# Key tiles of the last token group and the gates beside them, moved from one PSUM tag to another

## The chip, the cores and the metric

The kernel runs on one core of a Trainium2 chip. The metric is the device time of one execution in microseconds (us), given as the median of several executions. A profile of one execution records what each engine did: TensorE (PE in the profile, its weight loads PEld), VectorE (DVE), ScalarE (ACT), GpSimd (POOL) and SyncE (SP), which here issues the DMAs.

## What is computed

The program is a trunk of two layers over 1024 latent tokens and 256 context tokens of width 1024. Cut to what matters here, a layer is:

```python
h = _rms(x) * (1 + scale) + shift            # hc likewise for the context tokens
fa, za, u, vs, zb, q, k, va, zc, g = _split_proj(h @ w_in[l])
q = _axial_rope(_qk(q, N_HEADS, q_norm_g[l]), row, col)
k = _axial_rope(_qk(k, N_KV_HEADS, k_norm_g[l]), row, col)
attn = _latent_attn(q, k, va, kc, vc, attn_sink[l])       # window of 3 blocks, the context, a sink
ga, gb, gc = jnp.split(jax.nn.sigmoid(g), 3, axis=-1)
merged = ga * (ya @ w_pa) + gb * (yb @ w_pb) + gc * (yc @ w_pc)
x = x + gate * (merged @ w_out)
```

ya and yb come from a Fourier mixer and a gated mixer that the change doesn't touch. The context tokens go through the first layer in full, and in the second give keys and values alone.

## The kernel before, in words

**Products.** Every product of a layer's input with a weight is made of three matmuls per block of 128 input channels (L237 to L239, `mm3`), since both operands are split into a high and a low part. A product over 1024 channels is therefore 24 matmuls. `proj_tm` (L246) makes a tile of 128 tokens by 256 columns, `proj_cm` (L241) one of 128 columns by up to 512 tokens. A weight is loaded as a granule (L207): a DMA into a buffer `raw` (two of them), a cast on ACT into `whi` (L212) and a subtraction on DVE into `wlo` (L213); there are five buffers each of `whi` and `wlo`, and a new granule waits until the last matmul on the granule whose buffer it takes.

**PSUM.** A product needs one of eight banks. The pool of line 98 gives them out by tag: two for `mm` (products), three for `s` (scores), two for `pt` (transposes) and one for `o`. `bank(tag)` takes a tile of a tag. A tile whose tag has no free bank waits until all that read and write the tile before it in that bank are done; this holds up the first matmul into it, and PE issues in order, so all that stands behind it waits too.

**The stage in question** is the first part of `attention` (L462 to L496), once in each layer. It goes over three token groups: the context ("C", 256 tokens), then "0" and "1" (512 tokens each). Each block of 128 tokens gets a *key tile*: `proj_tm`, then `qk_norm_rope` (L306) on the key half and two reads of the value half (L484 on ACT, L485 on DVE). `qk_norm_rope` is a long chain through four engines: squares on ACT with the result back in the same bank (L311), scale and power on POOL (L312, L313), a multiplication on DVE that reads the bank (L316), the rotation on POOL and DVE (L325 to L336), and a transpose on PE (L486). The bank comes free with L316, L484 and L485. The input `H[g]` of a group is made just before (`modulate`, L272), in the first layer and, for the last group, in the second.

Beside the key tiles stand two other things. Before the last group ("1"), two *query tiles* are made (`prepare`, L455, `queries`, L435): they take `mm` banks and hold them much longer, since the transposed queries come back into the same bank (L441) and are read from there by ACT and DVE (L446, L447). And `early` (L465) gives *gates made ahead* (`ahead`, L634): `proj_cm`, a tanh on ACT that reads the bank (L644), a DMA of the result to DRAM (L645). In the first layer one follows each key tile, nine in all, of 256 context tokens; in the second there are four of 256 tokens, beside the last group alone.

After the stage come the units of attention: scores into `s` banks (L362 to L371), maxima on DVE, exponentials on ACT (L378, L379), the division on POOL (L387), transposes into `pt` (L399), values into `o` (L406, L407), with more products on `mm` as fill, three more gates among them (`lead`, L617).

**Who sets the order.** The program is written in this order, but each engine's queue is filled by a scheduler when the program is built. It keeps an estimate of its own of when each bank comes free, so a change of tags moves instructions on all engines.

**Which bank a tile takes.** The tiles of the stage that matter: key tiles alternate between the two tags (L479: `bank("mm" if ib % 2 else "s")`), and `ahead` always takes `mm` (L641). So the two `mm` banks serve the two query tiles, half of the key tiles and all gates made ahead.

Of the kernel before, what the change touches and what calls it, by code (L numbers as in the profile page):

```python
# [20 lines left out]
CTX = 256  # L21
# [45 lines left out]
def trunk_kernel(ctx: ExitStack, tc: tile.TileContext, a: dict, out: bass.AP):  # L67
# [17 lines left out]
    def bank(tag):  # L85
        tags = banks["tags"]
        tag = tag if tag in tags else "g"
        return banks["pool"].tile([128, 512], F32, tag, bufs=tags[tag])
# [127 lines left out]
    def w_cm(l, c0):  # L216

        return granule(a["w_in"][l, :, c0:c0 + 128].rearrange("(k p) c -> p k c", p=128), [128, KC, 128])
# [22 lines left out]
    def proj_cm(o, wg, h, n):  # L241

        for k in range(KC):
            mm3(o[:, :n], wg[0][:, k, :], wg[1][:, k, :], h[0][k], h[1][k], k == 0, k == KC - 1)

    def proj_tm(o, wt, h, t0):  # L246

        for k in range(KC):
            wh, wl = wt[k // 4]
            mm3(o[:, 0:256], h[0][k][:, t0:t0 + 128], h[1][k][:, t0:t0 + 128],  # L250
                wh[:, k % 4, :], wl[:, k % 4, :], k == 0, k == KC - 1)
# [167 lines left out]
    def attention(l, groups, sideA, sideB, xp, wkv, X, S):  # L419
# [13 lines left out]
        blocks = [(g, GROUPS[g][0] // 128 + i) for g in groups for i in range(GROUPS[g][1] // 128)]  # L433
# [21 lines left out]
        def prepare(u):  # L455
            kv, g, t, pr = units[u]
            if (kv, t) not in Q:
                if kv not in W:
                    W[kv] = w_tm(a["w_in"][l], C_Q + kv * 256)
                Q[kv, t] = queries(W[kv], g, t)  # L460

        wt = wkv or w_tm(a["w_in"][l], C_KV)  # L462
        ib = 0
        names = ("C", "0", "1")
        early = Fill(before_work(l, groups, S, se["pool"]))  # L465
        if X:
            modulate(l, "C", X["C"], xp)
        for ig, g in enumerate(names):
            if ig == 2:
                prepare(0)  # L470
                prepare(2)
            if X and ig < 2:
                modulate(l, names[ig + 1], X[names[ig + 1]], xp)
            g0, n = GROUPS[g]
            pk = bank("pt")
            for i in range(n // 128):
                t = g0 // 128 + i
                ib += 1
                p = bank("mm" if ib % 2 else "s")  # L479
                proj_tm(p, wt, H[g], i * 128)  # L480
                kf = qk_norm_rope(p, 2, 2, rope, None if g == "C" else t, np_)
                pv = p[:, 128:256].rearrange("p (g d) -> p g d", g=2)

                ACT.mul(vt[:, t, :, 0:64], pv, 0.5)  # L484
                DVE.scalar_tensor_tensor(vt[:, t, :, 64:128], pv, 0.5, vt[:, t, :, 0:64].bitcast(F32), ALU.mult, ALU.subtract)  # L485
                PE.transpose(pk[:, i * 128:(i + 1) * 128], kf[:, 0:128], ident)  # L486
                if "C" in groups:
                    early.upto(early.done + 1)
                elif ig == 2:
                    early.upto(early.done + 1)  # L490
            for kv in range(2):
                src = pk[kv * 64:(kv + 1) * 64, :n]
                hi = kk[0:64, kv, g0:g0 + n]
                ACT.copy(hi, src)
                DVE.tensor_tensor(kk[64:128, kv, g0:g0 + n], src, hi.bitcast(F32), ALU.subtract)
# [6 lines left out]
        st = Pool(tc, name="sd", bufs=1, side=sideB)  # L502
# [41 lines left out]
    def stored(S, key, n):  # L544
        S[key] = dp.tile([128, n], F32, "d" + "_".join(map(str, key)))
        return S[key]

    def staged(st, n=512):
        if st is not se["pool"]:
            return st.tile([128, 512], F32, "st", bufs=stores["n"])[:, :n]  # L550
        return st.tile([128, CTX], F32, "se", bufs=2)[:, :n]
# [69 lines left out]
    def before_work(l, groups, S, st):  # L621

        if "C" in groups:
            return ahead(l, context_blocks(range(9)), S, st)
        return ahead(l, [(b, 1, "0") for b in (0, 2)], S, st, CTX)

    def few(gen, n):
        for _ in range(n):
# [2 lines left out]
    def context_blocks(r):  # L631
        return [(i % 3, i // 3, "C") for i in r]

    def ahead(l, blocks, S, st, part=None):  # L634

        for b, j, g in blocks:
            w = w_cm(l, C_G + b * D + j * 128)
            o = stored(S, ("T", b, j, g), GROUPS[g][1])
            n = part or GROUPS[g][1]
            for c in range(0, GROUPS[g][1], n):  # L640
                p = bank("mm")  # L641
                proj_cm(p, w, [[y[:, c:c + n] for y in x] for x in H[g]], n)
                s = staged(st, n)
                ACT.activation(s, p[:, :n], AF.Tanh, scale=0.5)  # L644
                nc.sync.dma_start(o[:, c:c + n], s)  # L645
                yield n
# [333 lines left out]
    for l in range(DEPTH):  # L980
# [6 lines left out]
        S = {}  # L987

        wkv = None if l else wkv
        attention(l, groups, A, B, xp, wkv, None if l else X, S)  # L990
        stores["n"] = 5
        if not last:
            bigs["C"].close()
        st = Pool(tc, name="st", bufs=1, side=A)
# [5 lines left out]
        blocks = [(b, 0, g) for b in (0, 2) for g in lat]  # L1000
# [130 lines left out]
```

## Time and profile before

| | |
|---|---|
| time, median of 3 executions (lowest, highest) | 1948.63 us (1947.56, 1950.77) |
| the profiled execution's own time | 1947.46 us |
| its span in the profile | 1945.7 us |
| busy: PE, PEld, DVE, ACT, POOL | 1888.2, 1639.1, 1083.1, 798.4, 610.6 us |
| mean granted TensorE clock | 0.992 |
| idle time of PE in the whole span | 1945.7 - 1888.2 = 57.5 us |

A row of the waits view reads "who waited <- for whom: us in total, times, longest". A timeline row reads "start, duration, engine, line, operation, out<-in, how often [idle before <- what ended it]". In a row of the windows view the engines' busy times stand in the order of its heading, each with its number of instructions, and after them the granted clock. Names of tiles are the program's, without their numbers. The stage lies at about 43 to 145 us in the first layer and at about 1097 to 1160 us in the second.

### The profile page before, as it was taken

Reading aid. Unit: us, or ns where it says so; the run is one execution under the profiler, and the core shown is the slowest. Engines: PE = TensorE matmul, PEld = TensorE weight load, DVE = VectorE, ACT = ScalarE, POOL = GpSimd, SP = SyncE. Lnnn points to the kernel's source line nnn. Section 1 sums busy time; section 2 is a strip of 40 time slices with the busy share of each in tenths; the row PEclk is TensorE's granted clock in tenths of the full one; section 3 lists DMA queues with packets and bytes.
Section 4 is the critical chain, followed back from the end, with each engine's and each line's share of the span. In section 5 each row is a group of like instructions: output and inputs, shape, how many; then the busy total and the mean of one; then the engine's idle time right before and its main releaser. Section 6 shows DMA issues by size and latency. Waiting matters only on the chain.

```text
span 1945.7 us, 31000 instructions
## 1 busy us (share of the span) xinstructions
PE 1888.2 (97%) x10975; PEld 1639.1 (84%) x10975; DVE 1083.1 (56%) x2175; ACT 798.4 (41%) x2088; POOL 610.6 (31%) x975
## 2 busy tenths in 40 slices
PE   7889999999999999999999989999999999999998
PEld 2888999999988887888878978899888888888887
DVE  4565665556655548766355556666665655622242
ACT  2654555445644422111243445555554443111221
POOL 1564344443231112121124454334432021211122
PEclk9999999999999999999999999999999999999999
DMA  9332122213554667554374412112124568633362
GB/s 331 105 101 64 50 68 61 72 47 95 162 185 152 191 214 244 164 171 148 120 259 152 136 55 66 57 59 84 34 87 152 155 194 264 201 93 98 127 220 103
DMA packets 270610, 259.77 MB, mean 134 GB/s; under 512 B 20792, under 2 KB 213496, under 8 KB 270456
## 3 DMA queue, kind: packets, MB, share of 16 engines
q1 hardware_dynamic: 270456, 257.80, 41.9%
q8 instruction: 86, 1.41, 0.3%
q14 instruction: 68, 0.56, 0.1%
HBM read 196.91 MB, written 60.83 MB: 132 GB/s over the span
## 4 chain that ended last, share of the span: by engine, by line
PE 82%; DMA 6%; DVE 5%; ACT 3%; issue 2%; POOL 2%; SPq 1%; POOLq 0%; ACTq 0%; DVEq 0%
PE mm L237 16%; PE mm L238 16%; PE mm L239 16%; PE s L238 6%; PE s L237 6%; PE s L239 6%; PE pt L399 3%; DMA raw<-in_w_in_dram 2%; PE o L407 2%; PE o L406 2%; PE s L371 2%; PE s L364 1%; PE s L365 1%; DVE wlo L213 1%; DMA lt<-dT 1%
## 5 line engine op out<-in xcount | busy, mean ns | idle before, releaser
L213 DVE TENSOR_TENSOR wlo<-raw,whi 128x1024 fp32r<-128x1024 f32 (+2 forms) x210 | 243.3, 1161 | 216.3 <-ACT whi L212 207.5
L212 ACT CAST whi<-raw 128x1024 fp32r<-128x1024 f32 (+2 forms) x210 | 202.7, 967 | 363.7 <-PE s L238 139.2
L237 PE MATMUL mm<-hh,whi 128*128 128x512 f32 (+1 forms) x752 | 292.4, 389 | 5.6 <-DVE st L562 3.8
L238 PE MATMUL mm<-hl,whi 128*128 128x512 f32 (+1 forms) x752 | 291.1, 387 | 0.0
L239 PE MATMUL mm<-hh,wlo 128*128 128x512 f32 (+1 forms) x752 | 290.7, 387 | 0.0
L237 PE MATMUL mm<-whi,hh 128*128 128x256 f32 (+1 forms) x704 | 217.6, 309 | 8.1 <-DVE qt L447 5.2
L685 POOL TENSOR_TENSOR m<-m,tb 128x512 f32<-128x512 f32 x64 | 87.1, 1363 | 412.0 <-DVE tb L684 367.6
L239 PE MATMUL mm<-whi,hl 128*128 128x256 f32 (+1 forms) x704 | 214.7, 305 | 0.0
L238 PE MATMUL mm<-wlo,hh 128*128 128x256 f32 (+1 forms) x704 | 214.7, 305 | 0.0
L237 PEld LDWEIGHTS mm<-hh,whi 128*128 128x128 f32 x752 | 141.3, 188 | 33.3 <-DVE st L562 4.7
L239 PEld LDWEIGHTS mm<-hh,wlo 128*128 128x128 f32 x752 | 141.3, 188 | 27.3
L238 PEld LDWEIGHTS mm<-hl,whi 128*128 128x128 f32 x752 | 141.4, 188 | 25.6
L237 PEld LDWEIGHTS mm<-whi,hh 128*128 128x128 f32 x704 | 135.5, 192 | 14.7 <-issue 5.6
L387 POOL TENSOR_SCALAR P<-P,rd 128x640 f32<-128x640 f32 (+2 forms) x144 | 115.0, 809 | 102.1 <-DVE rd L385 63.9
L238 PEld LDWEIGHTS mm<-wlo,hh 128*128 128x128 f32 x704 | 135.7, 193 | 5.0
L239 PEld LDWEIGHTS mm<-whi,hl 128*128 128x128 f32 x704 | 135.4, 192 | 4.8
L238 PE MATMUL s<-hl,whi 128*128 128x512 f32 x352 | 137.5, 391 | 0.0
L237 PE MATMUL s<-hh,whi 128*128 128x512 f32 x352 | 137.4, 390 | 0.0
L239 PE MATMUL s<-hh,wlo 128*128 128x512 f32 x352 | 137.2, 390 | 0.0
L269 DVE TENSOR_TENSOR pl<-pt,ph 128x512 fp32r<-128x512 f32 (+1 forms) x184 | 112.0, 615 | 27.4 <-ACT ph L268 25.0
L268 ACT CAST ph<-pt 128x512 fp32r<-128x512 f32 (+1 forms) x184 | 95.8, 535 | 28.0 <-PE o L406 15.8
L196 DVE SCALAR_TENSOR_TENSOR aacc<-araw,scol,aacc 128x256 f32<-128x256 f32 x196 | 102.2, 554 | 5.1 <-DMA araw<-in_w_ada_dram 2.7
(303 smaller groups left out, 4435.0 us busy)
## 6 DMA issues: line engine op xcount, KB each, us to landing
raw<-in_w_in_dram SPq DMA_DIRECT2D x122, 512.0 KB, 4.1
araw<-in_w_ada_dram SPq DMA_DIRECT2D x48, 512.0 KB, 6.0
raw<-in_w_out_dram SPq DMA_DIRECT2D x40, 512.0 KB, 3.8
dP<-st SPq DMA_DIRECT2D x64, 256.0 KB, 2.3
lp<-dP SPq DMA_DIRECT2D x64, 256.0 KB, 4.2
x<-in_x_dram SPq DMA_DIRECT2D x16, 512.0 KB, 8.6
raw<-in_w_pc_dram SPq DMA_DIRECT2D x32, 256.0 KB, 2.9
dM<-m SPq DMA_DIRECT2D x32, 256.0 KB, 3.4
```

The costliest lines, as they stand in the source:

```text
L196: DVE.scalar_tensor_tensor(acc[:, v, :], raws[k // 4][:, k % 4, :], sc, acc[:, v, :], ALU.mult, ALU.add)
L212: ACT.copy(hi, raw)
L213: DVE.tensor_tensor(lo, raw, hi.bitcast(F32), ALU.subtract)
L237: PE.matmul(o, lh, rh, start=start, stop=False)
L238: PE.matmul(o, lh, rl, start=False, stop=False)
L239: PE.matmul(o, ll, rh, start=False, stop=stop)
L268: ACT.copy(hi, src)
L269: DVE.tensor_tensor(lo, src, hi.bitcast(F32), ALU.subtract)
L371: PE.matmul(bc[:, h * 256:h * 256 + 256], qt[:, s, 2 * pr + h, :], kk[:, g, SEQ:NTOK], start=(h + s == 0), stop=(s == 1), skip_group_check ...
L387: POOL.tensor_scalar(P[hh][:, :nl + 256], P[hh][:, :nl + 256], rd[:, hh:hh + 1], 1.0, ALU.mult, ALU.mult)
L399: PE.transpose(b[:, (2 * i + hh) * 128:(2 * i + hh + 1) * 128], P[hh][:, (i0 + i) * 128:(i0 + i + 1) * 128], ident)
L685: POOL.tensor_tensor(m, m, s, ALU.add)
```

## The change

The key tiles of the last group all take the tag `s`, and so do the gates that `before_work` hands out (nine in the first layer, four in the second). The gates made ahead elsewhere (`lead`, and those after attention) keep `mm`. No product, weight, DMA or reader is added or taken away.

```diff
-                p = bank("mm" if ib % 2 else "s")
+                p = bank("mm" if ib % 2 and ig < 2 else "s")
...
         if "C" in groups:
-            return ahead(l, context_blocks(range(9)), S, st)
-        return ahead(l, [(b, 1, "0") for b in (0, 2)], S, st, CTX)
+            return ahead(l, context_blocks(range(9)), S, st, tag="s")
+        return ahead(l, [(b, 1, "0") for b in (0, 2)], S, st, CTX, "s")
...
-    def ahead(l, blocks, S, st, part=None):
+    def ahead(l, blocks, S, st, part=None, tag="mm"):
...
-                p = bank("mm")
+                p = bank(tag)
```

What this does to the queues, at three places. A tile keeps its number when it changes its tag: 1027 and 1072 are the first layer's query tiles; 1118, 1197, 1276 and 1355 its key tiles of the last group; 1169, 1248 and 1327 the last three of its nine gates. In the second layer 12720 and 12772 are the query tiles, 12825, 12904, 12976 and 13055 the key tiles, 12876, 12948, 13027 and 13099 the gates.

First, PE in the first layer, around the transposes of the first query tile (L441), before:

```order
L239 MATMUL mm_1072<-whi_1023,hl1C_294 128x256
L486 MATMUL pt_694<-ident_69,qf_964 128x128
L441 MATMUL mm_1027<-ident_69,qf_1061 128x128 x2
L237 MATMUL mm_1118<-whi_243,hh01_602 128x256
L238 MATMUL mm_1118<-wlo_244,hh01_602 128x256
L239 MATMUL mm_1118<-whi_243,hl01_604 128x256
```

and now:

```order
L238 MATMUL s_1248<-hl0C_293,whi_1243 128x256
L239 MATMUL s_1248<-hh0C_291,wlo_1244 128x256
L441 MATMUL mm_1027<-ident_69,qf_1061 128x128 x2
L237 MATMUL s_1248<-hh1C_292,whi_1243 128x256
L238 MATMUL s_1248<-hl1C_294,whi_1243 128x256
L239 MATMUL s_1248<-hh1C_292,wlo_1244 128x256
```

Before, the key tile 1118 stands right behind L441 and takes the bank that the query tile leaves; now 1118 stands 120 matmuls earlier, and L441 lies inside a gate.

Second, PE in the second layer, at the same transposes, before:

```order
L239 MATMUL mm_12772<-whi_12716,hl10_11963 128x256
L362 LDWEIGHTS identb_74
L362 MATMUL s_13196<-maskb_87,identb_74 128x128
L486 MATMUL pt_12527<-ident_69,qf_12648 128x128
L486 MATMUL pt_12527<-ident_69,qf_12692 128x128
L441 MATMUL mm_12720<-ident_69,qf_12754 128x128 x2
L237 MATMUL mm_12825<-whi_12438,hh01_12328 128x256
L238 MATMUL mm_12825<-wlo_12439,hh01_12328 128x256
```

and now:

```order
L238 MATMUL s_12948<-hl00_11962,whi_12871 128x256
L239 MATMUL s_12948<-hh00_11960,wlo_12872 128x256
L441 MATMUL mm_12720<-ident_69,qf_12754 128x128 x2
L237 MATMUL s_12948<-hh00_11960,whi_12871 128x256
L238 MATMUL s_12948<-hl00_11962,whi_12871 128x256
```

The first scores (L362) and the key tile 12825 are no longer next to L441; a key tile and most of a gate now stand between the end of the second query tile and L441.

Third, ACT in the first layer, where a gate hands its bank to a key tile (the gate 1248, then the key tile 1276), before:

```order
L212 CAST whi_1437<-raw_1435 128x1024
L311 ACTIVATE mm_1276,s2_1301<-mm_1276 128x64
L311 ACTIVATE s_1355,s2_1380<-s_1355 128x64
L644 ACTIVATE se_1273<-mm_1248 128x256
L409 COPY ot_1623<-o_1609 64x256
```

and now:

```order
L446 CAST qt_1065<-mm_1027 64x2x128 x2
L212 CAST whi_1322<-raw_1320 128x1024
L644 ACTIVATE se_1273<-s_1248 128x256
L311 ACTIVATE s_1197,s2_1222<-s_1197 128x64
L484 ACTIVATE vt_283<-s_1118 128x2x64
```

Before, the gate and the key tile lay in different banks, and the reading of the gate's tile (L644) stood behind the key tile's own squares; now the cast of the next gate's weights (L212) stands just ahead of it, and the next key tile's first matmul stands right behind the gate's last on PE.

## The prediction

> **What bounds the kernel now.** The page comes first.
>
> ```profile
> span 1945.7 us, 31000 instructions
> PE 1888.2 (97%) x10975; PEld 1639.1 (84%) x10975; DVE 1083.1 (56%) x2175; ACT 798.4 (41%) x2088; POOL 610.6 (31%) x975
> PE 82%; DMA 6%; DVE 5%; ACT 3%; issue 2%; POOL 2%; SPq 1%; POOLq 0%; ACTq 0%; DVEq 0%
> ```
>
> PE works for 97% of the span and is 82% of the chain that ended last. The change alters no product, so the time can move in two ways alone: by PE's idle time, and by the clock at which its matmuls run. The windows view shows both. Its first two rows hold the stage in each layer; the other three are single products.
>
> ```profile
> core 0: us, PE busy (x) PEld busy (x) DVE busy (x) ACT busy (x) POOL busy (x), PEclk, DMA share, GB/s
> 75.00:165.00 90.00, 79.41 (x611) 76.11 (x611) 53.73 (x126) 48.51 (x157) 52.70 (x101) 0.98 0.30 89
> 1125.00:1160.00 35.00, 27.47 (x204) 26.01 (x203) 19.90 (x58) 14.59 (x60) 20.20 (x47) 0.90 0.14 43
> 109.80:114.50 4.70, 4.70 (x27) 4.70 (x28) 0.31 (x1) 0.00 (x1) 1.46 (x3) 0.64 0.00 0
> 1136.00:1141.60 5.60, 5.42 (x28) 5.38 (x28) 0.57 (x3) 0.38 (x2) 1.36 (x4) 0.58 0.00 0
> 1127.50:1130.60 3.10, 3.09 (x26) 3.04 (x27) 1.50 (x7) 0.16 (x2) 2.78 (x7) 1.00 0.00 0
> ```
>
> PE is idle for 90.00 - 79.41 = 10.6 us in the first layer's stage and for 35.00 - 27.47 = 7.5 us in the second's, 18.1 us together. No other engine is busy for more than 60% there, and the DMA share is 0.30 and 0.14. So this is waiting, and PE's waits in these two stretches say for whom:
>
> ```profile
> PE mm L237 <- DVE qt L447: 2.6, 1, 2.6
> PE s L371 <- ACT P L379: 2.3, 1, 2.3
> PE mm L441 <- DVE qf L336: 2.2, 1, 2.2
> PE mm L237 <- DVE st L562: 1.1, 1, 1.1
> PE mm L237 <- DVE vt L485: 1.0, 1, 1.0
> PE mm L441 <- POOL qf L321: 0.8, 1, 0.8
> PE mm L237 <- ACT se L644: 0.6, 1, 0.6
> ...
> PE mm L237 <- DVE qt L447: 3.8, 2, 2.6
> PE mm L441 <- ACT kk L494: 2.2, 1, 2.2
> PE mm L237 <- DVE vt L485: 0.9, 2, 0.7
> PE mm L237 <- DVE ta L334: 0.3, 1, 0.3
> PE pt L486 <- DVE qf L336: 0.3, 1, 0.3
> ```
>
> Seven rows are the first layer's, five the second's. The form "PE mm L237" is the first matmul of a product on an `mm` bank. It waits for the last reader of the tile before it there: L447 is a query tile's, L485 a key tile's, L644 a gate's. Two timelines of PE show the largest:
>
> ```profile
> 106.98 0.27 PE L441 MATMUL mm<-ident,qf 128*128 128x128 f32 x1
> 109.81 0.50 PE L237 MATMUL mm<-whi,hh 128*128 128x256 f32 x1 [2.55 <-DVE qt L447]
> 110.11 0.41 PE L238 MATMUL mm<-wlo,hh 128*128 128x256 f32 x1
> ...
> 1133.13 0.41 PE L441 MATMUL mm<-ident,qf 128*128 128x128 f32 x2 [2.18 <-ACT kk L494]
> 1136.18 0.56 PE L237 MATMUL mm<-whi,hh 128*128 128x256 f32 x1 [2.65 <-DVE qt L447]
> ```
>
> In both layers a key tile takes the bank that a query tile has just left. PE transposes the queries (L441), ACT and DVE read them, and PE has nothing it may do until then.
>
> **What the change takes away.** The order answers for each wait.
>
> - *Query tile to key or gate* (2.6 and 3.8 us): key tiles of the last group and gates no longer use `mm`. In the new order the transposes L441 lie inside a gate, and no product within 80 instructions behind them needs the banks of the two early query tiles. Gone: 6.4 us.
> - *Waits for the query chain before L441* (0.8, 2.2 and, in the second layer, 2.2): the first layer's early query tile now has 120 instructions of PE between its last product and its L441 where it had 36, the later one 68 where it had 36. The second layer's has 119 where it had 87: the two that come in between are a key tile and most of a gate, and in the trace the rotated queries were ready at 1133.13, when PE now still works on these. At 3.10 / 26 = 0.119 us each, from the last row of the windows, 68 are 8.1 us. Gone: 5.2 us.
> - *The score behind L379* (2.3): the second context score took the bank of the first; now it takes a gate's, whose last matmul lies 32 instructions back. Gone: 2.3 us.
> - *Gates and key tiles behind a gate or a key tile on `mm`* (0.6 and 1.0 in the first layer; 0.9 - 0.7 = 0.2, 0.3 and 0.3 in the second): these are on three banks now with more distance. Gone: 2.4 us.
> - *Kept*: L562, a fill product that the change doesn't touch (1.1 us), and the 0.7 us wait of the second query tile for L485 in the second layer, up to which both orders agree.
>
> That is 6.4 + 5.2 + 2.3 + 2.4 = 16.3 us of idle time. The clock adds to it. After the two longest stops a product ran at a granted clock of 0.64 and 0.58. At 0.119 us each the 27 and 28 matmuls would have taken 3.2 and 3.3 us instead of 4.70 and 5.42: 1.5 + 2.1 = 3.6 us lost. I count this as gone with the stops: together 19.9 us.
>
> The Trainium skill, "TensorE: Matmul & The Clock Gate", section "What's actually happening", lets the clock drop only after an idle window of about 3.4 us. By that rule the stops of 2.55 and 2.65 us are too short to be the cause and the 3.6 us would stay. The rows speak against it, since both low stretches begin with the product right behind the stop; but 2.3 and 2.2 us stops had none.
>
> **What it adds.** The work of 13 gates and four of the eight key tiles moves to three `s` banks. New waits arise where the new order puts a tile closely behind the last matmul of the tile whose bank it takes. What it would wait for:
>
> ```profile
> 121.53 1.04 ACT L212 CAST whi<-raw 128x1024 fp32r<-128x1024 f32 x1
> 122.47 0.39 ACT L644 ACTIVATE se<-mm 128x256 f32<-128x256 f32 x1
> ...
> 114.13 0.28 PE L239 MATMUL mm<-whi,hl 128*128 128x256 f32 x1
> ...
> 117.96 0.28 DVE L485 SCALAR_TENSOR_TENSOR vt<-mm,vt 128x128 fp32r<-128x128 f32 x1
> ```
>
> A gate's bank comes free after 0.39 us of L644. But two gates have the next gate's cast (L212, 1.04 us) ahead of L644 on ACT, and that cast itself waits for the gate's last matmul: two granules of key weights and two of query weights hold four of the five buffers. The 0.6 us row above was waited for one L644, so a hand-over takes about 0.2 us beside it. Such a bank therefore comes free 1.04 + 0.39 + 0.2 = 1.6 us after the last matmul. A key tile's bank comes free about 118.24 - 114.41 = 3.8 us after its last matmul when nothing stands before it, 32 matmuls. The order has these close ones:
>
> - gate 1248 to key tile 1276, no distance: 1.6 us.
> - gate 1169 to key tile 1197, 8 instructions (1.0 us) between: 0.6 us.
> - a lead gate to a fill product on the same `mm` bank, 9 between, cast ahead: 0.5 us; that fill product to a query tile, 10 between: 1.1 us, the price of the L562 row.
> - later in the first layer, one fill product to the next, 6 between: 0.9 us by the same row.
> - second layer: one lead gate to a query tile, 8 between, with a cast ahead: 0.9 us. Key tile 12825 to 12976 has 80 matmuls (9.5 us) between, but its L485 now stands behind the queries' L447 on DVE: 0.3 us.
>
> Sum 5.9 us. From below each may be nothing, for the tiles' readers may run ahead of my reckoning; from above each may cost what the worst hand-over of the trace costs, 2.65 us, 18.6 us for seven. I take the sum, as the causes are those of its rows. ACT's squares of key tiles (L311) queue behind the casts, but the banks they hold are wanted 52 instructions later or more, 6.2 us against 3.8.
>
> **The queues.** The gates' DMAs move with them. SP meets one obstacle:
>
> ```profile
> 99.02 0.37 SPq L209 DMA_DIRECT2D raw<-in_w_in_dram  x1
> 121.45 0.34 SPq L427 DMA_DIRECT2D gain<-in_k_norm_g_dram  x1
> 122.88 0.36 SPq L645 DMA_DIRECT2D dT_C<-se  x1
> 123.85 0.38 SPq L209 DMA_DIRECT2D raw<-in_w_in_dram  x1
> ```
>
> The second layer's key gain waits 22 us for the last rotation table on POOL, with weight loads behind it. In the new order four issues that stood behind it stand ahead of it, two weight loads among them. The next load is wanted by ACT's cast before the first exponentials.
>
> ```profile
> raw<-in_w_in_dram SPq DMA_DIRECT2D x122, 512.0 KB, 4.1
> ```
>
> A load lands 4.1 us after its issue, and the DMA share in the stage is 0.30: I cost the queue at nothing. What covers it is 87 instructions, 10.4 us, that PE has in the new order between the first context score and the first L399. If a load came late by more than that, the exponentials behind the cast, and PE, would wait for the rest of it.
>
> **The sum.** 19.9 - 5.9 = 14.0 us. The profiled execution took 1947.46 us (span 1945.7 and 1.8 around it), so it would take 1933.5. The median of the runs is 1.2 us higher, 1948.63, so I predict 1934.6 us.
>
> **Rivals.**
>
> *The clock is not bound to these stops* (chance 0.13). For it: the stops of 2.3 and 2.2 us had no low clock, and the low stretches may fall elsewhere. Then 3.6 us less are gained: 10.4 us, 1938.2 us. The Trainium skill's rule on the clock gate, quoted above, would come out here.
>
> *What was waited for at the bank comes back at the softmax* (0.18). The first scores of each layer now stand behind all key tiles; the stage's fill is used up before them, and the chain from scores to L399 lies bare. For it: the new order does put the first layer's first context score 100 PE instructions later. Against: 10.4 us of matmuls still stand between it and L399. Should the chain take 5 us longer than that in each layer, 10 of the 14.0 us go back: 1944.6 us. Two thirds of this chance lie within 0.2% of no change.
>
> *The three `s` banks become the bound* (0.08, slower). Some 21 tiles of the two stages (thirteen gates, eight key tiles) now hand over `s` banks, while `mm` stands idle behind two query tiles. If each hand-over cost the 1.6 us reckoned for an adjacent gate, that is 33.6 us against 19.9 gained: 13.7 us slower, 1962.3 us. It turns at 19.9 / 21 = 0.95 us each. Against: most have 24 or more matmuls between. The Trainium skill, "Perfetto Trace Analysis", section "Matmuls", would have independent products rotate through different banks so that the reading of one overlaps the next; fewer banks for more products goes against it.
>
> That the change does nothing is excluded by the order.
>
> **How the numbers follow.** The forecast itself, a gain of about 8 to 20 us, has 0.61. A measurement of this kernel can tell about 0.2%, 3.9 us, from no change. Faster: 0.61 + 0.13 + 0.06 = 0.80; same: 0.12; slower: 0.08. The low end, 1927, is all of 19.9 us with the kept 1.8 gone too and no new wait; the high end, 1944, takes in new waits of about 15 us, near the bound, and leaves out most of the softmax rival and the slower one.
>
> **What would show it right or wrong.** Right: PE's idle time in the two stages falls from 18.1 to about 8 us; no wait "PE mm L237 <- DVE qt L447" is left there; new rows "PE s L237 <- ACT se L644" of 1 to 2 us appear; no granted clock under 1 in the stage. Wrong: waits of PE for P (L399) or for scores' banks (L362, L371) of several us at the end of the stage; rows "PE s L237 <- DVE vt L485" repeated; or the low clock at other places with the stops gone.

## The result, and the profile after

| | before | after |
|---|---|---|
| time, median of 4 executions each (lowest, highest) | 1948.62 us (1947.56, 1950.77) | 1930.79 us (1928.94, 1933.80) |
| ratio to before, 95% interval | | 0.9909 (0.9892 to 0.9925) |
| the profiled execution, its span | 1947.46, 1945.7 us | 1932.49, 1930.7 us |
| idle time of PE in the span | 57.5 us | 1930.7 - 1884.7 = 46.0 us |
| mean granted TensorE clock | 0.992 | 0.995 |

The kernel is 17.8 us faster; 14.0 were forecast. Two unaltered copies, run later with the experiments, gave 0.9919 and 0.9915. Two single executions of kernels further down took far longer than all others (6601.22 us with the queries moved, 2045.28 us with all key tiles on `mm`); the medians given there contain them, the ratios leave them out.

The page of the kernel after: span, engines, and the shares of the chain that ended last.

```profile
span 1930.7 us, 31006 instructions
PE 1884.7 (98%) x10975; PEld 1636.6 (85%) x10975; DVE 1083.1 (56%) x2175; ACT 796.3 (41%) x2088; POOL 608.5 (32%) x975
PE 81%; DMA 8%; DVE 4%; POOL 2%; ACT 2%; issue 2%; SPq 1%; POOLq 0%; DVEq 0%; ACTq 0%
```

The number of instructions of PE is the same. Its busy time fell by 1888.2 - 1884.7 = 3.5 us (the clock), its idle time by 11.5 us. The windows view of the kernel after, for the stage in the first layer and in the second; the columns are those of the heading in the prediction:

```profile
75.00:160.00 85.00, 81.07 (x612) 77.18 (x611) 53.80 (x126) 44.94 (x151) 53.16 (x102) 0.98 0.31 94
1116.00:1151.00 35.00, 33.31 (x255) 31.64 (x255) 23.81 (x62) 16.45 (x59) 22.06 (x47) 1.00 0.29 85
```

The first row holds as many PE instructions as the 90 us of before (612 against 611), the second 255 where 35 us of before held 204. PE is idle for 85.00 - 81.07 = 3.9 and 35.00 - 33.31 = 1.7 us: 5.6 us where there were 18.1, in the second layer over more work than before. The waits view of the kernel after says for what, the first five rows in the first layer (75 to 165 us), the other three in the second (1107 to 1160 us):

```profile
PE s L237 <- ACT se L644: 1.7, 1, 1.7
PE pt L399 <- POOL P L387: 1.3, 1, 1.3
PE o L406 <- ACT ph L268: 0.3, 1, 0.3
PE s L371 <- ACT P L379: 0.2, 1, 0.2
PE o L407 <- DVE pl L269: 0.2, 1, 0.2
...
PE mm L237 <- DVE vt L485: 0.9, 1, 0.9
PE s L237 <- DVE vt L485: 0.8, 1, 0.8
PE mm L441 <- DVE nm L375: 0.6, 1, 0.6
```

"PE mm L237 <- DVE qt L447", 6.4 us in three stops before, is in neither stretch. The score behind L379 went from 2.3 to 0.2 us, and of the waits before L441 one of 0.6 us is left, of a query tile that is not one of the early ones. Two new stops are over 1 us, and the timeline of the kernel after shows both:

```profile
109.31 1.04 ACT L212 CAST whi<-raw 128x1024 fp32r<-128x1024 f32 x1
110.38 0.38 ACT L644 ACTIVATE se<-s 128x256 f32<-128x256 f32 x1
110.82 0.39 PE L237 MATMUL s<-whi,hh 128*128 128x256 f32 x1 [1.68 <-ACT se L644]
...
138.43 2.06 POOL L387 TENSOR_SCALAR P<-P,rd 128x256 f32<-128x256 f32 x2
138.96 0.34 PE L399 MATMUL pt<-ident,P 128*128 128x128 f32 x1 [1.26 <-POOL P L387]
```

The first is the forecast's largest new wait, gate 1248 to key tile 1276: the cast of the next gate's weights stands ahead of the tanh on ACT, and 1.68 us pass where 1.6 were reckoned. The second was not in the sum: PE is through with its fill and waits for the division of the softmax.

**Where the 17.8 us lie.** To compare the two kernels over the same work I take two stretches between places that both orders share: from PE's 65th matmul to its 1727th (the first layer's stage and what surrounds it), and from the 6465th to the 7575th (the second's), counted in the order of time. Before:

```profile
37.05:280.67 243.62, 227.82 (x1663) 213.12 (x1663) 150.54 (x348) 138.46 (x422) 120.59 (x221) 0.98 0.31 92
1115.72:1287.90 172.18, 163.05 (x1113) 148.82 (x1112) 107.49 (x264) 92.95 (x312) 78.29 (x153) 0.98 0.21 63
```

and after:

```profile
36.07:272.94 236.87, 228.25 (x1663) 212.74 (x1663) 150.97 (x347) 137.49 (x424) 118.12 (x221) 0.98 0.32 96
1107.05:1270.95 163.90, 160.21 (x1112) 146.65 (x1111) 107.50 (x264) 92.66 (x313) 79.16 (x153) 1.00 0.22 66
```

In the second layer 172.18 - 163.90 = 8.3 us went: idle time from 9.13 to 3.69 (5.4 us), and busy time from 163.05 to 160.21 (2.8 us), with the granted clock up from 0.98 to 1.00. In the first layer 6.8 us went: idle time fell by 7.2 us (15.80 to 8.62), and busy time rose by 0.4. Together these are 15.0 us. The first stretch also begins 1.0 us sooner (36.07 for 37.05), the work between the two stretches took 0.9 us less, and what follows the second took 2.0 us more, so the two profiled executions differ by 15.0 us in all. The remaining 2.8 us of the 17.8 lie in which executions were profiled: that of before was 1.2 us under its median and that of after 1.7 us above. The experiments show that the first was lucky in its first layer.

### The profile page after: what moved, and what is told of

It reads as the page before. It is cut to its first block, busy times and chain, and to the rows that moved or that the text cites. A ratio compares the mean times of both kernels' runs of the same rounds, so it can differ in the third digit from the quotient of the medians.

```text
span 1930.7 us, 31006 instructions
## 1 busy us (share of the span) xinstructions
PE 1884.7 (98%) x10975; PEld 1636.6 (85%) x10975; DVE 1083.1 (56%) x2175; ACT 796.3 (41%) x2088; POOL 608.5 (32%) x975
## 4 chain that ended last, share of the span: by engine, by line
PE 81%; DMA 8%; DVE 4%; POOL 2%; ACT 2%; issue 2%; SPq 1%; POOLq 0%; DVEq 0%; ACTq 0%
PE mm L237 15%; PE mm L238 15%; PE mm L239 15%; PE s L238 6%; PE s L237 6%; PE s L239 6%; PE pt L399 3%; DMA raw<-in_w_in_dram 2%; PE o L406 2%; PE o L407 2%; PE s L371 2%; PE s L364 1%; PE s L365 1%; DVE wlo L213 1%; DMA lt<-dT_C 1%
## 5 line engine op out<-in xcount | busy, mean ns | idle before, releaser
L213 DVE TENSOR_TENSOR wlo<-raw,whi 128x1024 fp32r<-128x1024 f32 (+2 forms) x210 | 243.1, 1160 | 218.4 <-ACT whi L212 213.4
L212 ACT CAST whi<-raw 128x1024 fp32r<-128x1024 f32 (+2 forms) x210 | 202.7, 967 | 374.1 <-PE s L238 146.2
L237 PE MATMUL mm<-hh,whi 128*128 128x512 f32 x720 | 284.2, 395 | 2.9 <-DVE st L562 2.7
L238 PE MATMUL mm<-hl,whi 128*128 128x512 f32 x720 | 282.8, 393 | 0.0
L239 PE MATMUL mm<-hh,wlo 128*128 128x512 f32 x720 | 282.6, 392 | 0.0
L237 PE MATMUL mm<-whi,hh 128*128 128x256 f32 (+1 forms) x672 | 206.6, 307 | 2.2 <-ACT st L644 1.1
L239 PE MATMUL mm<-whi,hl 128*128 128x256 f32 (+1 forms) x672 | 204.4, 304 | 0.0
L238 PE MATMUL mm<-wlo,hh 128*128 128x256 f32 (+1 forms) x672 | 204.1, 304 | 0.0
L237 PEld LDWEIGHTS mm<-hh,whi 128*128 128x128 f32 x720 | 135.8, 189 | 30.4 <-DVE st L562 3.9
L238 PE MATMUL s<-hl,whi 128*128 128x512 f32 (+1 forms) x384 | 146.8, 382 | 0.0
L237 PE MATMUL s<-hh,whi 128*128 128x512 f32 (+1 forms) x384 | 146.7, 382 | 0.0
L239 PE MATMUL s<-hh,wlo 128*128 128x512 f32 (+1 forms) x384 | 146.4, 381 | 0.0
L237 PEld LDWEIGHTS mm<-whi,hh 128*128 128x128 f32 x672 | 127.9, 190 | 8.1 <-ACT st L644 1.6
L238 PEld LDWEIGHTS mm<-wlo,hh 128*128 128x128 f32 x672 | 128.0, 190 | 5.0
```

The source lines that it names most:

```text
L212: ACT.copy(hi, raw)
L213: DVE.tensor_tensor(lo, raw, hi.bitcast(F32), ALU.subtract)
L237: PE.matmul(o, lh, rh, start=start, stop=False)
L238: PE.matmul(o, lh, rl, start=False, stop=False)
L239: PE.matmul(o, ll, rh, start=False, stop=stop)
```

## The experiments

The **theory**: before, a product that PE reaches soon had to take a bank which a query tile held through its long chain, and PE stood still for the rest of that chain; with query tiles and short products on different tags, this can't happen. The first **rival**: it is a matter of how many tiles share the two `mm` banks, so that each tile taken away gives its small part. The second: the gain comes from the instructions' new places.

### One part alone: the key tiles

```diff
-                p = bank("mm" if ib % 2 else "s")
+                p = bank("mm" if ib % 2 and ig < 2 else "s")
```

The gates stay on `mm`.

> Only the key tiles of the last group go to the scores' tag; the gates made ahead stay with the products' tag. Theory (a stop arises where a key tile or gate has to take the bank that a query tile is still using): in the first layer no product stands within 13 instructions of PE behind the one whose bank it takes any more, so its stage gains as much as with the whole change or 1.7 us more (no gate hands a bank to a key tile), about 8 us; in the second layer one gate still stands right behind the first query tile's transposes, so a stop of about 2.6 us stays there, and the stage gains about 5 us instead of 8.4. In all about 1936 us. Rival (the gain is shared by the parts in proportion to the tiles that leave the products' tag): 4 of 17 tiles, so 4 us, 1944 us.

Measured: 1940.42 us, ratio 0.9953 (0.9940 to 0.9967), some 9 us faster. The theory had expected 13 and the rival 4, so the size decides nothing; the places say more. In the first layer no wait for L447 is left, and its stretch takes 237.99 us where the shown profile of before has 243.62. In the second layer the query tile is now followed in its bank by a gate, as the timeline of PE shows:

```profile
1129.30 0.28 PE L239 MATMUL s<-whi,hl 128*128 128x256 f32 x1
1129.42 0.38 PE L441 MATMUL mm<-ident,qf 128*128 128x128 f32 x2
1133.09 0.55 PE L237 MATMUL mm<-hh,whi 128*128 128x256 f32 x1 [3.29 <-DVE qt L447]
```

This is the stop of before with another product in the key tile's place, and longer; the stretch of this layer takes 168.42 us, against 172.18 before and 163.90 with the change. Four tiles off the tag gave half of the gain, but the stop stays where the order still puts a short product right behind a query tile in its bank.

### The other part alone: the gates

```diff
-            return ahead(l, context_blocks(range(9)), S, st)
-        return ahead(l, [(b, 1, "0") for b in (0, 2)], S, st, CTX)
+            return ahead(l, context_blocks(range(9)), S, st, tag="s")
+        return ahead(l, [(b, 1, "0") for b in (0, 2)], S, st, CTX, "s")
```

The key tiles keep their alternation.

> Only the gates made ahead go to the scores' tag; the last group's key tiles go on alternating between the tags. Theory: the key tiles that stay with the products' tag now have the query tiles alone beside them, and the order puts none right behind a query tile's transposes, so the stops of 2.5 us go in both layers; in the second layer two tiles stand 0 and 4 instructions behind a gate on the same bank, 0.6 to 1.6 us each. About 6 us in each layer, 1937 us. Rival (in proportion to the tiles that leave the products' tag): 13 of 17, so 14 us, 1935 us; the two differ by layer: the rival has the second layer, with 4 of 8 tiles moved, gain half of what the whole change gains there.

Measured: 1933.71 us, ratio 0.9922 (0.9909 to 0.9936), some 15 us faster, more than the theory's 12 and near the rival's 14. By layer the two come apart: the rival had the second layer gain half of what the change gains there, and its stretch is as short as with the whole change (163.90):

```profile
1111.17:1274.38 163.21, 159.90 (x1113) 146.81 (x1112) 107.45 (x265) 93.43 (x316) 82.73 (x154) 1.00 0.21 66
```

The waits view has no row of L447 in either layer, although key tiles and query tiles still share `mm`. The timeline of the first layer shows why:

```profile
111.72 0.38 PE L441 MATMUL mm<-ident,qf 128*128 128x128 f32 x2
114.34 0.38 PE L441 MATMUL mm<-ident,qf 128*128 128x128 f32 x2
114.48 0.36 PE L237 MATMUL mm<-whi,hh 128*128 128x256 f32 x1
```

The first row is the first query tile's, the second the other one's. The key tile that takes the first one's bank now starts 2.8 us behind its transposes, with part of a gate and of another key tile between, and waits for nothing. So here the shared tag by itself cost nothing; what cost time before was an order that put the next product of the tag close behind the query tile.

The parts don't add: 9 and 15 alone, 16 to 18 together. That speaks for a stop that needs both a query tile and a product close behind, and that goes as soon as the close product is elsewhere; in the orders that arise here it costs more to leave the gates on `mm` than to leave the keys.

### The opposite edit: only the query tiles move

```diff
-                prepare(0)
-                prepare(2)
+                prepare(0, "s")
+                prepare(2, "s")
```

with the tag handed through `prepare` to `queries`. Keys and gates are as before.

> The opposite edit: key tiles and gates stay as in the kernel before, and only the two query tiles made inside each stage take their banks from the scores' tag. Theory: it is the pairing of a long-held query tile with short products in two banks that costs, not the load on the products' tag; so the same stops go, and the adjacent gate and key tile of the changed kernel (1.7 us) are not there either: 1929 to 1931 us, as fast as the changed kernel or 2 us faster. Rival (it matters that products get a third bank in turn): products keep two banks, so nothing or little is gained, 1945 to 1949 us.

Measured: 1932.61 us, ratio 0.9910 (0.9895 to 0.9925): the same gain as the change, though no key tile and no gate has left `mm`. The waits view of this kernel, first layer (55 to 165 us) and second:

```profile
PE mm L237 <- DVE vt L485: 1.5, 1, 1.5
PE mm L237 <- ACT st L644: 0.5, 1, 0.5
...
PE mm L237 <- DVE vt L485: 1.1, 1, 1.1
PE mm L441 <- DVE nm L375: 0.6, 1, 0.6
```

No row of L447. Four tiles moved one way do what seventeen moved the other way did. The rival that counts tiles falls; the theory holds. The second rival, the instructions' new places, can't be set apart in full, since every edit here changes the tags and the order together, and the run of the gates shows that the order alone can put the products far enough apart.

### More of it: all key tiles of the last group on `mm`

```diff
-                p = bank("mm" if ib % 2 else "s")
+                p = bank("mm" if ib % 2 or ig == 2 else "s")
```

> Edit: the opposite dose. The last token group's key tiles that had the scores' tag go to the products' tag too, so that all of them, the gates and the query tiles share its banks; nothing else changes from the kernel before. The theory (a short product is handed the bank that a query tile still holds) expects more of the same stops: in layer 0 three more query-tile and key hand-overs within nine TensorE instructions, in layer 1 the key tile mm_12825 only 5 instructions behind mm_12720 and the gate mm_12876 only 10 behind mm_12772. At 1.0 to 2.6 us a stop and some 1.7 us for each half-clock stretch behind one: 4 to 10 us more than before, so 1953 to 1959 us. The rival (what counts is how many products are on the tag of the scores, each giving the same few tenths) expects the 8.8 us that the key tiles alone gave, spread over the tiles moved the other way, about as much: 1957. The rival that the gain came from where the instructions happened to fall expects no sign: 1949 +- 3.

Measured: 1954.70 us, ratio 1.0020 (1.0009 to 1.0031), 3.9 us slower by the ratio: the sign of the theory, the size just under the 4 to 10 us expected. This kernel's longest wait in the first layer, and the longest of the second:

```profile
PE mm L237 <- DVE qt L447: 2.4, 1, 2.4
...
PE pt L486 <- DVE qf L336: 2.8, 1, 2.8
PE s L364 <- POOL qt L449: 2.8, 1, 2.8
PE mm L237 <- DVE vt L485: 2.0, 1, 2.0
PE mm L237 <- DVE nm L375: 1.6, 1, 1.6
```

The first layer still has its stop at L447. In the second it is gone: the order put other work behind the query tiles, and the time was lost at other places of the same chain (a key's transpose, the scaling of the queries L449). The stretches say the same: 245.45 us in the first layer, no more than other profiles with the old first layer have (243.62 to 246.72), and 177.07 in the second, 5 us above before. So the loss lies where the hand-overs that I named did not come, and a worse order explains it as well as the sharing of the tag does. The run doesn't contradict the theory, and it doesn't bear it out either.

### One layer alone

The edit is the change with the tag made to depend on the layer, for instance

```diff
-                p = bank("mm" if ib % 2 else "s")
+                p = bank("mm" if ib % 2 and (l or ig < 2) else "s")
```

for the first layer.

> Edit: the change in layer 0 alone; layer 1's key tiles and early gates keep the products' tag. In the profiles of the changed kernel the stage of layer 0 was 6.0 us shorter and that of layer 1 8.2 to 8.3, 14.3 together, while the medians differ by 17.8. If the two layers add and the missing 3.5 us lie at the program's start, where the first early gates stand, this kernel gains 9.5 and the one with layer 1 alone 8.3. If the 3.5 us are the chance of which half-clock stretches fell into the one profile of the kernel before, this kernel gains 6.0 to 8.5 (in a second profile of the kernel before, layer 0's stage was 232 us in place of 229) and layer 1's the same 8.3.

> Edit: the change in layer 1 alone; layer 0 is as before. The theory expects layer 1's stops (2.18 and 2.65 us, and 1.16 behind them) and the half-clock stretch of 6.83 us gone, and layer 0's stops as they were: 8.3 us, 1941 to 1943. A rival (a layer alone gives less, as the stops of one layer move those of the next by shifting loads) expects the two single-layer kernels to gain together clearly less than the change, under 14 us.

Measured: the first layer alone 1938.25 us, ratio 0.9936 (0.9924 to 0.9948), 12.5 us by the ratio (10.1 to 14.8); the second alone 1942.94 us, ratio 0.9967 (0.9954 to 0.9981), 6.4 us (3.7 to 9.0). Together 18.9 us; the changed kernel in the same batch gained 16.6 us (ratio 0.9915, 0.9902 to 0.9928). They add, within the intervals. The first layer's part is larger than any of its expectations. A part of the reason is in the profiles of kernels whose first layer is that of before. A second profile of the kernel before and one of the kernel with the second layer alone have in the first stretch:

```profile
36.59:283.17 246.58, 229.22 (x1664) 214.70 (x1663) 150.36 (x347) 138.59 (x422) 120.84 (x221) 0.97 0.30 91
```

```profile
37.94:284.66 246.72, 229.78 (x1663) 215.20 (x1663) 150.33 (x347) 138.48 (x422) 120.67 (x221) 0.97 0.30 89
```

The same instructions take 229.22 and 229.78 us of busy time where the profile shown first had 227.82, and PE reaches its 1727th matmul at 283.17 and 284.66 us, not at 280.67. The mean of the three is 282.8 us; the four profiles with the change in this layer have 272.94, 273.22, 273.98 and 271.76, mean 273.0. That is 9.9 us. The second layer's stretch is steadier: 172.18, 171.69 and 171.99 without the change, 163.90, 163.97, 163.79 and 163.75 with it, 8.1 us. 9.9 + 8.1 = 18.0 us, close to the gain of the medians. (12.5 us, the first layer's part by the ratio, is more than 9.9, which lies just under its interval; that difference stays open.)

Over all fourteen profiles the stretches sort by the stop at L447. In the first layer the four kernels that have it take 243.6 to 246.7 us and the ten that don't 232.2 to 238.7. In the second the four that have it take 168.4 to 172.2 and nine that don't 162.5 to 164.0; the tenth is the kernel with all key tiles on `mm`, with 177.1.

### The kernel before once more

> The kernel before, unaltered, one more profile: the stops of the stage return to within 0.1 us each (2.55 and 2.65 us the two longest), and the stage of layer 0 is 229 us long within 0.5, that of layer 1 172. If a half-clock stretch is bound to the stop ahead of it, the three at 51.8, 109.9 and 1133.9 us return; if stretches come and go with something that a program does not set, at least one is missing or has moved.

Measured: 1948.72 us in its one execution. The stops came back (2.5 us at L447 in the first layer; in the second 2.39 where it had been 2.65), but from the first gate to the 1727th matmul of PE it took 232.1 us, not 229. The three half-clock stretches (a granted clock of 0.50) came back too, the first at half its length, and the first layer has two more. What differs is the clock, and the windows view shows what it goes with. I cut the time into slots of 3.41 us such that the half-clock stretches fill whole slots. The first profile of before, two pairs of slots and then the one pair behind L441 of the later query tile:

```profile
106.45:109.86 3.41, 0.49 (x3) 0.29 (x3) 2.39 (x5) 2.13 (x10) 2.05 (x4) 1.00 0.00 0
109.86:113.28 3.42, 3.42 (x16) 3.42 (x17) 0.25 (x1) 0.00 (x0) 1.40 (x3) 0.50 0.00 0
113.28:116.69 3.41, 1.82 (x16) 1.58 (x14) 1.35 (x5) 1.99 (x12) 1.22 (x4) 1.00 0.00 0
116.69:120.10 3.41, 2.66 (x22) 2.66 (x23) 3.31 (x11) 1.21 (x6) 3.24 (x9) 1.00 0.00 0
147.41:150.82 3.41, 1.85 (x16) 1.88 (x17) 3.26 (x7) 0.90 (x3) 2.55 (x3) 1.00 0.27 82
150.82:154.24 3.42, 3.42 (x30) 3.42 (x30) 1.05 (x3) 0.76 (x2) 1.20 (x2) 1.00 0.67 199
```

The second profile, the same work:

```profile
106.38:109.79 3.41, 0.86 (x8) 0.78 (x7) 2.17 (x5) 1.48 (x6) 2.42 (x4) 1.00 0.00 0
109.79:113.21 3.42, 3.42 (x18) 3.42 (x17) 0.00 (x0) 0.00 (x0) 0.73 (x1) 0.50 0.00 0
113.21:116.62 3.41, 1.13 (x10) 0.89 (x8) 1.97 (x8) 2.67 (x15) 1.92 (x6) 1.00 0.00 0
116.62:120.03 3.41, 3.36 (x15) 3.36 (x16) 3.37 (x13) 0.71 (x4) 3.18 (x10) 0.50 0.02 5
147.34:150.75 3.41, 1.03 (x10) 0.85 (x9) 2.80 (x5) 1.47 (x4) 2.52 (x4) 1.00 0.44 140
150.75:154.16 3.41, 3.41 (x18) 3.41 (x18) 1.65 (x5) 0.40 (x2) 1.70 (x3) 0.50 0.54 149
```

PE's busy time in a slot (the second number) goes with the clock of the next slot (the third number from the end). Busy for 0.49, 0.86, 1.13 and 1.03 us of 3.41, the next slot has 0.50; busy for 1.82 and 1.85 us, the next has 1.00. The limit is not sharp: a slot of the changed kernel that was busy for 1.78 of 3.40 us was followed by 0.51. The two stops of 2.3 and 2.2 us without a low clock, which the prediction could not explain, were spread over two slots each in the first profile; in the second they lay mostly within one.

The second layer in the first profile, two slots in a row:

```profile
1130.45:1133.86 3.41, 0.91 (x7) 0.42 (x5) 2.35 (x6) 2.48 (x11) 2.79 (x6) 1.00 0.00 0
1133.86:1137.27 3.41, 1.09 (x5) 1.12 (x6) 2.44 (x7) 0.45 (x2) 2.54 (x5) 0.50 0.00 0
```

Here the half clock begins at 1133.86 us, inside the 2.65 us stop, which ends at 1136.18. The slot ahead of it holds the 2.18 us wait for L441.

### Without the cast ahead of the tanh

The changed kernel with the early gates' casts on POOL (`pool` is true for gates on the tag `s`; the rest of the edit hands it down):

```diff
-        ACT.copy(hi, raw)
+        if pool:
+            POOL.tensor_scalar(hi, raw, 1.0, 0.0, ALU.mult, ALU.add)
+        else:
+            ACT.copy(hi, raw)
```

> Edit: the changed kernel, with the cast of the early gates' weights (L212) on GpSimd in place of ScalarE. My reading of the changed kernel's longest stop (1.68 us, the key tile s_1276 waits for the gate s_1248's tanh on ScalarE, L644) is that the cast of the next gate's weights stands ahead of that tanh on ScalarE. With the cast elsewhere the tanh starts as soon as its product is done: the stop falls to a matmul's drain and one tanh, about 0.5 us, and the kernel gains 1.0 to 1.3 us, 1932.0 where the changed kernel gave 1933.3. The rival (the wait is the tanh itself and its way to TensorE, one instruction being too short a distance) expects the stop to stay at 1.4 us or more, and 1933.3. A third way: GpSimd's cast is long enough to hold the keys' rotation there (L321, L387) and the kernel becomes slower, 1935 to 1938, with stops behind POOL.

Measured: 1937.26 us, ratio 0.9934 (0.9913 to 0.9955): no gain on the changed kernel (0.9909 to 0.9919 in its three batches), perhaps a loss; the intervals overlap. The stop did go, as the timeline shows (L647 and L240 are L644 and L237 of the others, L213 is the cast):

```profile
112.13 0.38 ACT L647 ACTIVATE se<-s 128x256 f32<-128x256 f32 x1
112.29 1.06 POOL L213 TENSOR_SCALAR whi<-raw 128x1024 fp32r<-128x1024 f32 x1
112.57 0.38 PE L240 MATMUL s<-whi,hh 128*128 128x256 f32 x1 [0.47 <-ACT se L647]
```

0.47 us in place of 1.68: the cast was the cause of the 1.2 us between them. But POOL carries the rotation of the keys and the division of the softmax already; it is busy for 628.9 us now where the changed kernel has 608.5. The waits of the first layer (55 to 165 us; L409, L402 and L291 are L406, L399 and L288):

```profile
PE o L409 <- ACT ph L271: 2.3, 2, 1.6
PE pt L402 <- POOL P L390: 1.5, 2, 1.2
PE pt L291 <- DVE x L287: 0.9, 1, 0.9
```

The changed kernel has 0.3, 1.3 and nothing in these places. The 1.2 us won at the bank were lost again at the softmax and at the input, and the first layer's stretch takes 238.7 us where the changed kernel's three profiles have 236.9 to 237.5; the third way of the expectation is the one that came, though POOL itself is the releaser in only one of the three rows. In the second layer, at 1170.93 us, PE waits 2.51 us for the division on POOL, which it doesn't in the changed kernel; the stretch there is no longer for it (163.4 us).

### Queries and six gates on the scores' tag

The kernel with the two early query tiles on `s`, and the first six early gates of the first layer there too, so that the 1.5 us wait in the waits of the queries-only kernel above has no shared bank left.

```diff
-            return ahead(l, context_blocks(range(9)), S, st)
+            return ahead(l, context_blocks(range(9)), S, st, tags=iter(["s"] * 6 + ["mm"] * 3))
```

> Edit: the two early query tiles on the scores' tag, and of the nine early gates of layer 0 the first six as well; the last three gates, the keys and layer 1's gates stay on the products' tag. The theory expects the one long stop left in the kernel with only the queries moved, 1.47 us at 59.8 us where the gate mm_570 waits for the bank of a value product (DVE vt L485), to go, since that gate has another bank, and no gate late enough to meet the query tile in the scores' banks: 1.5 us, with a half-clock stretch of 3.41 us behind it another 1.7, so 1929.4 to 1931.1 where the queries alone gave 1932.6. The rival (nothing in the stage waits long enough to be worth anything now) expects 1932.6 within 1.5.

> The two early query tiles and the first six early gates of layer 0 on the scores' tag, unaltered, beside the changed kernel on one chip. If the 1.47 us stop that it lacks against the queries-only kernel, and the 1.68 and 1.26 us stops that it lacks against the changed kernel, are worth their length, it is 2 to 4 us below the changed kernel; if they are covered later, it is within 1 us of it.

Measured: 1930.07 us, ratio 0.9890 (0.9873 to 0.9907), and once more 1930.78 us, ratio 0.9906 (0.9891 to 0.9921). It is faster than the kernel before, and 2.5 us below the changed kernel of the same batch by the medians, with intervals that overlap. The two profiles have no stop over 1 us in the stage once its first gate has begun. So little is left to gain there, and whether this version beats the change is not settled.

### The changed kernel, unaltered

> The changed kernel once more, unaltered, for a second profile and as a yardstick for the other runs of this call. If the half-clock stretches are tied to the longest stops of PE, this profile has them at the same places as the first profile of the changed kernel (139 us and 1358 us); if they come by a window of the clock's own, they lie elsewhere or are missing, and the time moves by about 1.7 us for each. 1929 to 1934 us.

> The changed kernel, unaltered, as the yardstick of this batch: 17.8 us below the kernel before within 2. Its stops: 1.68 us at s_1276 and 1.26 us at the transposes of L399, within 0.1 us each. If the clock is set by how much TensorE worked in the 3.41 us slots of a clock that runs on its own, its half-clock stretches again start whole multiples of 3.413 us apart, each behind a slot in which it stood for half or more, and not all of them fall where they did.

Measured: 1933.31 us, ratio 0.9919 (0.9907 to 0.9931), and 1933.23 us, ratio 0.9915 (0.9902 to 0.9928). The stop at key tile 1276 was 1.69 us in both, the one at L399 1.27 and 1.26: the stops belong to the program. Of the half-clock stretches the one behind L399 (at 139.8 and 139.6 us) returned in both; the one at 1357.7 us was missing in the first copy, which had one at 737.1 us, and was back at 1358.2 in the second.

## Why the prediction was right, point by point

- **What is taken away.** All four groups of waits went as reckoned: the hand-over from query tile to key or gate (6.4 us), the query chain before L441 (5.2), the score behind L379 (2.3, of which 0.2 is left), gates and key tiles behind each other (2.4). The opposite edit shows that the cause of the longest stops was the one named, the bank handed from a query tile to a short product; the run of the gates adds that the two must also stand close in the order. Of the 1.8 us that were to stay, the L562 wait of 1.1 us went too; why was not looked into.
- **What is added.** 5.9 us were reckoned from seven close hand-overs. One of them came at its size (1.6 forecast, 1.68 measured, and the cast as its cause shown by the run that moved it). One was larger (key tile 12976: 0.3 forecast, 0.8 measured). The other five, 4.0 us together, did not show: none is among the waits of 0.2 us or more. In their place stand 1.3 us at L399 with some 0.7 us of small waits beside it and 0.6 us at L441. The sum is near the forecast because misses of both signs met in it, which is luck, not because each term was right. One of the five, the 0.9 us behind the second layer's lead gate, had also been reckoned without a reason for its size: 1.6 us less 8 instructions is 0.6.
- **The softmax rival** came true in small: "the chain from scores to L399 lies bare" cost 1.3 us in one layer and a half-clock stretch behind it, not 5 us in each.
- **The idle time** was to fall from 18.1 to about 8 us and fell to 5.6.
- **The clock.** Counted at 3.6 us, gone with the two longest stops. In the second layer 2.8 us of busy time did go, but the half clock there was read wrongly: it did not begin with the product behind the 2.65 us stop, as the prediction has it, but inside that stop, behind the slot with the 2.18 us wait. Both waits went, so the sum did not suffer. In the first the shown pair of profiles has none of it, since one 3.41 us stretch went and another came behind L399; over three and four profiles the first layer gained 9.9 us where the pair, with its start-up, has 7.7. The expectation "no granted clock under 1 in the stage" was wrong in the first layer. The rival that the clock is not bound to these stops is wrong as stated, and the reason I gave against it was too simple: the low clock goes with how much of a slot PE stands still.
- **The three `s` banks** did not become the bound: the one long wait there is the one of the cast.
- **The size.** 14.0 us forecast, 17.8 measured. The term that was too small is the net of the first layer: 9.5 + 1.5 - 4.7 = 6.3 us by the prediction's terms against 9.9 us over several profiles; the second layer's 6.8 + 2.1 - 1.2 = 7.7 us stand against 8.1. The single-layer runs put more on the first layer (12.5 and 6.4 us by the ratios).

## What to carry to other kernels

A tile that keeps its PSUM bank through a chain over several engines should not share a tag with short products that PE reaches soon after: here PE stood still for the rest of that chain, and it mattered little which of the two was moved away. Where the order left enough other work between the two, as in the run of the gates, the shared tag cost nothing. To find it, read which tile's last reader the first matmul of a product waits for, and test the reading by the opposite edit, which is often the smaller one. When a bank comes free late although its reader is short, look at what stands ahead of that reader on its engine, and at what the other engine already carries before moving that work there.

## What the runs showed of the hardware

The granted clock of TensorE is set in slots of 3.413 us on a grid of its own, which doesn't start with the kernel: within each profile the half-clock stretches begin whole multiples of 3.413 us apart and are 3.41 or 6.83 us long, that at the end of the span apart, and in three profiles of the changed kernel the stretch behind L399 begins at 139.15, 139.77 and 139.64 us. I counted PE's busy time in each slot of the fourteen profiles, from 30 us on. Of the slots at full clock with PE idle for over 60%, the next was at half clock in 30 of 30; at 50 to 60% idle in 9 of 12; at 40 to 50% in 5 of 29; at 20 to 40% in 5 of 177; under 20% in none of some 7460. What decides in the slots between 20 and 60% is not known. So a stop of 2 to 2.5 us cost up to 1.7 us more, or nothing, by where it falls. The Trainium skill, "TensorE: Matmul & The Clock Gate", section "What's actually happening", speaks of a free-running window of 3413 ns; the trace agrees with the length and with its running free. It speaks of an idle window, where a slot idle for a little over half was mostly enough here.

This can also account for times that differ by a microsecond or two between executions of one kernel with the same stops; only the profiled ones can be checked. The two profiles of the kernel before differ by 3.0 us in the first layer's stretch (243.62 and 246.58), so a comparison of two single profiles can be off by as much.
